# Where the operands of three matrix products lie in SBUF, modulo 256 bytes, and the order of their parts

## The chip, the cores and the metric

The kernel runs on one core of a Trainium2 chip. The metric is device time in microseconds (us). Engine names are those of the profile: PE is the matrix engine (TensorE), PEld its weight loads, DVE the vector engine, ACT the scalar engine, POOL GpSimd, SP the engine that issues most DMAs.

## The reference: one layer of a streaming encoder

A layer for 1024 new frames (prompt) and 64 frames of a running stream (sample), 1088 frames in all, in float32. Cut to what matters:

```
proj = rmsnorm(x) @ w_in                       # 1024 -> 5120
cb, cc, ch, q, k, v, ga, gb = split(proj)
ya = (cb * causal_conv(cc * ch)) @ w_conv_out  # 512 -> 1024
o  = band_attend(q, k, v, rel_bias)            # 8 heads of 64, own chunk + 8 earlier
yb = o @ w_attn_out                            # 512 -> 1024
x  = x + (sigmoid(ga) * ya + sigmoid(gb) * yb) @ w_out
x  = x + (silu(h @ w1) * (h @ w3)) @ w2        # h = rmsnorm(x), 1024 -> 2816 -> 1024
y  = rmsnorm(x)
```

## The kernel before

**Two-part operands.** Every float32 operand of a large product is kept as two parts of the type fp32r: *high* is ACT's cast of the value (L128), *low* is what DVE's subtraction leaves (L129); both are written by `split`. A product is then three matmuls: high x high, high x low, low x high. Each matmul on PE is a weight load (128 columns of 4 bytes) and a stream of 272 or 512 columns; the weight load of the next matmul runs while the present one streams.

**Where weight parts live.** `slots` (L147) hands out one part in a tile of the pool `ws` (eight tiles of 512 floats) and the other in one of eight slots of the row `low`: slot s begins at float 512 s + `at`. All tiles of `ws` have the same address modulo 256 bytes, and all slots with one `at` have the same. `pair` puts high into `ws` and low into `low`, `moving_pair` (v and the output projection, `at` 24) the other way round.

**The stages, in order of time.** (1) From 11 us: the value projection v, nine tiles of frames; xn (the normed frames, by 128) is the weight, w_v streams, 512 columns, eight blocks of 128 in depth (`v_tile`, L515 to L517: high x high, low x high, high x low). A tile's transposes (L459) stand between. (2) From 69 to 344 us: q, k, the convolution's inputs and most of gate b by a seven-product scheme (`run`, L269, 272 columns). (3) 344 to 573 us: ten blocks of the gates (`gate`, `product`, L333 to L335: four quarters of the frames of 272 columns, eight blocks deep), and between their matmuls attention: scores (L907, L908), softmax (DVE L865, ACT L875), transposes (L954), weighted values (`values`, L979: v is the weight, the transposed probabilities `pt` stream). The tile scheduler sets how the two interleave from their order in the program and their waits. Weights of a gate block, and of the next product after it, are loaded by SP and split by ACT and DVE ahead of use (`next_w`, `prep`). (4) 573 to 670 us: ya and yb, also by `product`, four blocks deep, `at` 40. (5) 670 to 771 us: the output projection in two halves of 512 columns (`wo_half`, `token_product`, L1163 to L1168: the merged activations `mg` are the weight, w_out streams). Frames tile 8, with 64 frames, takes two matmuls a block (L1167, L1168). The second half also adds the residual, norms and transposes. (6) To 1230 us: w_ff1 and w_ff3 by `run`. (7) To 1462 us: w_ff2 (L1682, 512 columns; L1509 for tile 8) and the final norm.

**Distances.** For a matmul that streams from address m while the weights of the next matmul are loaded from address w, call (w - m) modulo 256 bytes its distance. In the program as it is placed, the three matmuls of one block of depth have these distances, in the order of the lines:

| product | before | columns |
|---|---|---|
| v, and the output projection | 96, 192, 0 | 512 |
| weighted values | 64 | 512 and 256 |
| gates, quarters 0 and 2 | 96, 224, 0 | 272 |
| gates, quarters 1 and 3 | 192, 0, 192 | 272 |
| ya and yb, quarters 0 to 3 | 0, 0, 96; 192, 192, 32; 128, 128, 224; 64, 64, 160 | 272 |
| `run` (six matmuls a block) | 0, 192, 96, 0, 224, 192 | 272 |
| w_ff2 | 0, 0, 0 | 512 |

Of the kernel before, what the change touches and what calls it, by code (L numbers as in the profile page):

```python
# [8 lines left out]
F32 = mybir.dt.float32  # L9
# [6 lines left out]
P = 128  # L16
D = 1024
KD = D // P
# [15 lines left out]
HN = HT // 2  # L34
# [32 lines left out]
def encoder_kernel(ctx: ExitStack, tc: tile.TileContext, ins, outs):  # L67
    nc = tc.nc
    mm = nc.tensor.matmul
# [74 lines left out]
    def slots(nm, at):  # L144
        taken[0] += 1
        a = taken[0] % 8 * 512 + at
        return ws.tile([P, 512], F32R, tag="w", name=f"w{nm}"), low[:, a : a + 512]  # L147

    def pair(nm, at=0):
        return [t.rearrange("p (k n) -> p k n", k=4) for t in slots(nm, at)]  # L150

    def moving_pair(nm):
        lo, hi = slots(nm, 24)
        return hi, lo

    def quarters(nm):
        return Quarters(
# [146 lines left out]
    def prep(upto):  # L304
        while prep.n < min(upto, len(plan)):
            plain_load(prep.n)
            ld, kt, at = plan[prep.n]
            w = []
            for k in range(0, kt, 4):
                nm = f"p{prep.n}_{k}"  # L310
                hi, lo = pair(nm, ld.get("at", 0))
                split(hi, lo, ld["raw"][:, k : k + 4, at : at + P])
                w.append((hi, lo))
            plan[prep.n] = w
            prep.n += 1
# [10 lines left out]
    def product(out, w, x, o, n):  # L326

        kt = 4 * len(w)
        for k in range(kt):
            a, b = (t[:, k % 4] for t in w[k // 4])  # L330
            p, q = x.at(0, k, o, n), x.at(1, k, o, n)
            first, then = (q, p) if x is xn and o // HN % 2 == 0 else (p, q)
            mm(out, a, first, start=k == 0, stop=False)  # L333
            mm(out, a, then, start=False, stop=False)  # L334
            mm(out, b, p, start=False, stop=k == kt - 1)  # L335

    PIECES = [(j * HN, HN) for j in range(4)]
# [1 line left out]
    for g, m in GATES:  # L339
        if m % 2 == 0:  # L340
            base = (C_GA if g == "a" else C_GB) + m * P
            ld = {"src": w_in[:, base : base + 2 * P], "w": 2 * P}
# [10 lines left out]
    xn = quarters("xn")  # L353
# [53 lines left out]
    wv = []  # L407
# [99 lines left out]
    def v_tile(i):  # L507
        t0, n = TT[i]
        pv = bank1("BD", f"pvv{i}")[:, 0]
        for k in range(KD):  # L510
            if i == 8:
                a, b = xs8[:, k, :TS], xs8[:, k, TS:]
            else:
                a, b = xn.at(0, k, column(i), P), xn.at(1, k, column(i), P)
            mm(pv[:n], a, wv[k][0], start=k == 0, stop=False)  # L515
            mm(pv[:n], b, wv[k][0], start=False, stop=False)
            mm(pv[:n], a, wv[k][1], start=False, stop=k == KD - 1)  # L517
        put_v(slot(VST, D), pv, n, t0 if t0 < TP else TP + CACHE, nc.gpsimd)
        if t0 >= TP - CACHE:
            v32 = slot(V32, ATT)  # L520
            act.copy(v32[:n], pv[:n])
            if t0 < TP:
                dst = outs["cache_v_prompt"][t0 - (TP - CACHE) : t0 - (TP - CACHE) + n]
            else:
                dst = outs["cache_v_sample"][CACHE - TS :]
            nc.gpsimd.dma_start(dst, v32[:n])
# [278 lines left out]
    at_pool = att_stack.enter_context(tc.tile_pool(name="at_pool", bufs=2, reuse_waits="tile"))  # L805
# [115 lines left out]
    def transposed(h, t, s):  # L921
        tp = patt.tile([P, 2, 512], F32, tag="att", name=f"t{h}_{t}").rearrange("p a b -> p (a b)")
        if t == 8:
            pt = at_pool.tile([P, 2, 5, TS], F32R, tag="pts", name=f"pts{h}", bufs=1)
            for i in range(4):
                nc.tensor.transpose(
                    tp[:, i * TS : (i + 1) * TS], s[:TS, i * P : (i + 1) * P], ident[:TS, :TS]
                )
            nc.tensor.transpose(tp[:TS, 512 : 512 + TS], s[:TS, 512:576], ident[:TS, :TS])
            split(pt[:, 0, :4, :], pt[:, 1, :4, :], tp[:, : 4 * TS].rearrange("p (b t) -> p b t", t=TS))  # L930
            split(pt[:TS, 0, 4, :], pt[:TS, 1, 4, :], tp[:TS, 512 : 512 + TS])
            pts[h, 4] = pt

            sm = sums.pop(h)
            vec.reciprocal(sm, sm)
            tr = patt.tile([P, 2, 512], F32, tag="att", name=f"rt{h}")[:9, 0, :P]
            nc.tensor.transpose(tr, sm, ident)
            rows = at_pool.tile([P, P], F32, tag="rows", name=f"rows{h}", bufs=1)[:9]
            act.copy(rows, tr)
            for e in range(2):  # L940
                nc.gpsimd.dma_start(
                    rc_d[h, e * HT : e * HT + 512].rearrange("(t p) -> t p", p=P), rows[4 * e : 4 * e + 4]
                )
                c = e * HT + 512
                nc.gpsimd.dma_start(rc_d[h : h + 1, c : c + 32], rows[8:9, 32 * e : 32 * e + 32])
            return
        g, j = divmod(t, 2)
        if j == 0:
            pts[h, g] = at_pool.tile([P, 2, 6, 256], F32R, tag="pt", name=f"pt{h}_{g}")
        pt = pts[h, g]  # L950
        nb = min(t + 1, 5)
        b0 = t - nb + 1 - max(0, 2 * g - 4)
        for i in range(nb):
            nc.tensor.transpose(tp[:, i * P : (i + 1) * P], s[:, i * P : (i + 1) * P], ident)  # L954
        src = tp[:, : nb * P].rearrange("p (b t) -> p b t", t=P)
        js = slice(j * P, (j + 1) * P)
        split(pt[:, 0, b0 : b0 + nb, js], pt[:, 1, b0 : b0 + nb, js], src)
# [101 lines left out]
    for i in range(4, len(GATES)):  # L1059
        gate_w[i] = next_w()  # L1060
        if i == len(GATES) - LAST:
# [5 lines left out]
            for nm, pad in (("u", 56), ("ob", 48)):  # L1067
                uo.tile([P, pad], F32, name=f"pad_{nm}")
                t = uo.tile([P, 2, 4 * T + 8], F32R, name=nm)[:, :, : 4 * T]
# [10 lines left out]
            for k, r in zip((2, 3), late_r):  # L1080
                o = ob.t[:, 0, k].bitcast(F32)
                with tc.issue_after(u_ld.ins):
                    nc.sync.dma_start(o, o_d[k * P : (k + 1) * P])
                    ld = rc_load(r, k)
# [12 lines left out]
    for m0 in range(0, 8, 2):  # L1097
        for m in (m0, m0 + 1):
# [3 lines left out]
            for o, n in PIECES:  # L1102
                t = sg["ga", m, o]
# [5 lines left out]
        for m in (m0, m0 + 1):  # L1109
# [3 lines left out]
            for o, n in PIECES:  # L1113
                t, z = sg.pop(("ga", m, o)), sg.pop(("gb", m, o))
# [7 lines left out]
                h, a = o // HT, 512 - o % HT  # L1122
# [34 lines left out]
    def token_product(ps, i, x, kt, w, first=True, last=True):  # L1157

        for k in range(kt):
            wh, wl = w(k)  # L1160
            f, e = first and k == 0, last and k == kt - 1
            if i < 8:
                mm(ps, x(k, 0), wh, start=f, stop=False)  # L1163
                mm(ps, x(k, 1), wh, start=False, stop=False)  # L1164
                mm(ps, x(k, 0), wl, start=False, stop=e)  # L1165
            else:
                mm(ps, x(k, None), wh, start=f, stop=False)  # L1167
                mm(ps, x(k, None), wl, start=False, stop=e)  # L1168
# [21 lines left out]
    if True:  # L1190
# [7 lines left out]
        for i in ORDER:  # L1198
            t0, n = TT[i]
            xt = wp.tile([P, D], F32, tag="xg", name=f"xr{i}")[:, :512]  # L1200
            nc.sync.dma_start(xt[:n], x_rows(i)[:, :512])
            ps = bank2("BD", f"wo0_{i}")[:, 0]
# [369 lines left out]
    for n in range(1, len(names)):  # L1572
# [7 lines left out]
        if 2 <= n < 18:  # L1580
            nm, src = (("k", ck), ("v", cvv))[(n - 2) // 8]
            a = (n - 2) % 8 * 56
# [21 lines left out]
    bufs = {(hp, "hs"): 1, (hp, "snap"): 3, (hp, "sa"): 4, (hp0, "snap"): 1, (hp0, "sa"): 1}  # L1604
# [30 lines left out]
    q = 0  # L1635
    for b, ks in enumerate(blocks):
        first, final = b == 0, b == len(blocks) - 1
        nk = blocks[b + 1] if not final else []
        for g in range(2):
            ps = {}  # L1640
# [27 lines left out]
            for si, js in turns:  # L1668
                p, ht = STEPS[si], hts[base + si]
# [99 lines left out]
```

## Time and profile before

| | |
|---|---|
| median of 3 runs | 1471.76 us (1471.53 to 1471.95) |
| span of the profiled execution | 1470.3 us |
| PE busy | 1455.5 us, 99%, 10176 matmuls |
| PEld busy | 1366.9 us, 93% |
| DVE busy | 983.1 us, 67% |
| ACT busy | 679.7 us, 46% |
| DMA | 260 MB, 177 GB/s on average |

The profiled execution's own time is its span, 1470.3 us; 1.46 us of the median lie outside it. How to read the views: a group's row gives line, engine, operation, out<-in, tile sizes, count, busy time and the mean of one. A row by source line gives the shortest, median and longest of one in ns. A timeline row gives start, length and count; successive matmuls overlap in the timeline, since a matmul's row lasts until its last result is written, and the next has then begun to stream. What a matmul costs is the distance of its start from the next one's start, which is here called its spacing.

### The profile page before, as it was taken

The numbers are of one execution on the slowest core, as the hardware profiler recorded it, in microseconds if no ns is written. First come the engines' busy times: TensorE is split into PE (matmuls) and PEld (weight loads), VectorE is DVE, ScalarE is ACT, GpSimd is POOL, SyncE is SP. The second block draws the span as 40 slices with busy tenths as digits, with TensorE's granted clock in tenths as the row PEclk, the third lists the DMA queues.
The fourth block names the chain that finished last, engine by engine and source line by source line (L and its number), as shares of the span: only waits on it lengthen the run. The fifth ranks groups of instructions, "written<-read, shape, count | busy, mean of one in ns | idle before, by whom it ended". The sixth has DMA issues, their size and how long they took to land.

```text
span 1470.3 us, 26411 instructions
## 1 busy us (share of the span) xinstructions
PE 1455.5 (99%) x10176; PEld 1366.9 (93%) x10176; DVE 983.1 (67%) x1856; ACT 679.7 (46%) x1391; POOL 136.5 (9%) x249
## 2 busy tenths in 40 slices
PE   8999999999999999999999999999999999999997
PEld 6899999999989899998889999999999999888886
DVE  7975565641677775753588767666666768957677
ACT  7654333332777776531355444444444445512223
POOL 1400010001111111000100111110011111000000
PEclk9999999999999999999999999999999999999999
DMA  8687522237776657434432443443344448867686
GB/s 280 185 274 227 182 78 94 66 111 228 209 192 180 182 172 244 158 126 136 154 108 80 153 168 139 168 150 123 122 153 168 147 168 305 286 228 245 219 265 208
DMA packets 163133, 260.26 MB, mean 177 GB/s; under 512 B 18784, under 2 KB 98848, under 8 KB 163008
## 3 DMA queue, kind: packets, MB, share of 16 engines
q1 hardware_dynamic: 142080, 192.79, 41.6%
q0 software_dynamic: 19776, 63.70, 12.1%
q10 hardware_dynamic: 1152, 2.10, 0.4%
q8 instruction: 80, 1.31, 0.4%
q14 instruction: 45, 0.37, 0.1%
HBM read 170.67 MB, written 89.70 MB: 177 GB/s over the span
## 4 chain that ended last, share of the span: by engine, by line
PE 92%; DVE 3%; DMA 3%; ACT 1%; issue 1%; SPq 1%; ACTq 0%; DVEq 0%
PE Ab L269 9%; PE Aa L269 8%; PE A L1682 8%; PE Db L269 4%; PE Da L269 4%; PE D L1682 4%; PE Agb L269 2%; PE Bb L269 2%; PE Ba L269 2%; PE B L1682 2%; PE wo L1163 2%; PE wo L1165 2%; PE wo L1164 2%; PE g L335 2%; PE g L334 2%; PE g L333 2%
## 5 line engine op out<-in xcount | busy, mean ns | idle before, releaser
L333 PE MATMUL g<-xn,wp 128*128 128x272 f32 x320 | 93.7, 293 | 0.0
L335 PE MATMUL g<-xn,low 128*128 128x272 f32 x320 | 93.4, 292 | 0.0
L334 PE MATMUL g<-xn,wp 128*128 128x272 f32 x320 | 92.7, 290 | 0.0
L128 ACT CAST ring<-w2r 128x512 fp32r<-128x512 f32 (+1 forms) x78 | 43.2, 588 | 98.4 <-PE A L1682 50.7
L865 DVE CUSTOM_DVE_ANT_0 p<-s,bb 128x640 f32<-128x640 f32 (+5 forms) x72 | 47.5, 660 | 38.5 <-DMA qd<-q_d 26.2
L1682 PE MATMUL A<-ring,low 128*128 128x512 f32 x264 | 72.3, 389 | 0.0
L1682 PE MATMUL A<-ring,ht 128*128 128x512 f32 x264 | 72.3, 390 | 0.0
L129 DVE TENSOR_TENSOR low<-rawa,wa 128x512 fp32r<-128x512 f32 x55 | 37.7, 687 | 41.7 <-ACT wa L128 41.7
L335 PEld LDWEIGHTS g<-xn,low 128*128 128x128 f32 x320 | 60.3, 188 | 0.5
L333 PEld LDWEIGHTS g<-xn,wp 128*128 128x128 f32 x320 | 60.3, 188 | 0.5
L334 PEld LDWEIGHTS g<-xn,wp 128*128 128x128 f32 x320 | 60.2, 188 | 0.5
L1682 PEld LDWEIGHTS A<-ring,ht 128*128 128x128 f32 x264 | 49.4, 188 | 10.6 <-ACT acc L1692 0.4
L1682 PEld LDWEIGHTS A<-ring,low 128*128 128x128 f32 x264 | 49.6, 188 | 10.3
L269 PE MATMUL Ab<-tt,wb 128*128 128x272 f32 x352 | 57.8, 285 | 1.3 <-ACT wb L128 1.3
L129 DVE TENSOR_TENSOR ring<-w2r,ring 128x512 fp32r<-128x512 f32 (+1 forms) x78 | 49.0, 646 | 13.4 <-ACT ring L128 13.2
L269 PE MATMUL Ab<-mg,wb 128*128 128x272 f32 x352 | 58.0, 285 | 0.0
L269 PE MATMUL Aa<-tt,wa 128*128 128x272 f32 x352 | 57.8, 285 | 0.0
L269 PE MATMUL Aa<-mg,wa 128*128 128x272 f32 x352 | 57.7, 285 | 0.0
L875 ACT ACTIVATE p<-p,mx 128x640 f32<-128x640 f32 (+5 forms) x72 | 50.8, 706 | 11.4 <-DVE mx L865 10.1
L128 ACT CAST wa<-rawa 128x512 fp32r<-128x512 f32 x55 | 34.0, 621 | 47.4 <-PE Ab L269 33.3
L128 ACT CAST wb<-rawb 128x512 fp32r<-128x512 f32 x55 | 34.0, 620 | 38.7 <-PE Aa L269 24.5
L1163 PE MATMUL wo<-low,mg 128*128 128x512 f32 x128 | 50.9, 397 | 0.0
(554 smaller groups left out, 4547.9 us busy)
## 6 DMA issues: line engine op xcount, KB each, us to landing
h_d<-hq POOLq DMA_DIRECT2D x44, 512.0 KB, 4.4
ht<-h_d SPq DMA_DIRECT2D x77, 256.0 KB, 3.9
low<-h_d SPq DMA_DIRECT2D x77, 256.0 KB, 3.7
h_d<-hq_early POOLq DMA_DIRECT2D x29, 512.0 KB, 4.6
rawa<-in_w_ff SPq DMA_DIRECT2D x11, 1024.0 KB, 6.2
rawb<-in_w_ff SPq DMA_DIRECT2D x11, 1024.0 KB, 5.5
w2r<-in_w_ff SPq DMA_DIRECT2D x11, 1024.0 KB, 7.9
qd<-q_d SPq DMA_DIRECT2D x32, 272.0 KB, 4.1
```

The source lines that it names most:

```text
L128: a = act.copy(hi, src)
L129: b = vec.tensor_tensor(lo, src, hi.bitcast(F32), op=ALU.subtract)
L269: newest[0] = mm(t[:, j, :HN], w[:, k, :], x[p][:, k, l, j * HN : (j + 1) * HN], start=p in (1, 2, 7) and k == 0 and n == 0, stop=k == 3 a ...
L333: mm(out, a, first, start=k == 0, stop=False)
L334: mm(out, a, then, start=False, stop=False)
L335: mm(out, b, p, start=False, stop=k == kt - 1)
L865: vec.tensor_tensor_reduce(out=s if len(ps.shape) == 2 else s.rearrange("p (a b) -> p a b", a=2), in0=ps, in1=bias if len(ps.shape) == 2 e ...
L875: act.activation(s, s, AF.Exp, bias=mx, scale=-1.0, accum_out=sm)
L1163: mm(ps, x(k, 0), wh, start=f, stop=False)
L1164: mm(ps, x(k, 1), wh, start=False, stop=False)
L1165: mm(ps, x(k, 0), wl, start=False, stop=e)
L1682: mm(t, ht[k][:, j, x], w[:, l], start=p in (1, 2, 7) and k == 0 and n == 0, stop=k == len(ks) - 1 and n == 2, skip_group_check=p in (6, 5 ...
```

## The change

Four edits.

1. `moving_pair` (v and the output projection) now puts high into `ws` and low into `low`, with `at` 48 instead of 24. In `v_tile` and `token_product` the order becomes high-high, high-low, low-high (the first word for the weights).
2. Gate weights (the products with eight blocks of depth) are swapped: high into `low`, low into `ws`, and their `at` is 44 instead of 0. The last gate block's slot in `low` (floats 3116 to 3627) and the slot of the first block of ya (3624 to 4135, `at` 40) then share four floats, so four columns of the last gate block's last block of depth hold other numbers when they are read.
3. `product` no longer streams xn's low part first in the even quarters of the gates.
4. A tile of 16 floats in front of `pt` moves the probabilities by 64 bytes.

The distances as the changed program is placed; the others stay:

| product | before | after |
|---|---|---|
| v, and the output projection | 96, 192, 0 | 0, 0, 0 |
| weighted values | 64 | 0 |
| gates, quarters 0 and 2 | 96, 224, 0 | 144, 96, 144 |
| gates, quarters 1 and 3 | 192, 0, 192 | 80, 32, 80 |

```diff
     def moving_pair(nm):
-        lo, hi = slots(nm, 24)
-        return hi, lo
+        return slots(nm, 48)
...
                 nm = f"p{prep.n}_{k}"
-                hi, lo = pair(nm, ld.get("at", 0))
+                hi, lo = pair(nm, ld.get("at", 44))
+                if kt == KD:
+                    hi, lo = lo, hi
                 split(hi, lo, ld["raw"][:, k : k + 4, at : at + P])
...
             p, q = x.at(0, k, o, n), x.at(1, k, o, n)
-            first, then = (q, p) if x is xn and o // HN % 2 == 0 else (p, q)
-            mm(out, a, first, start=k == 0, stop=False)
-            mm(out, a, then, start=False, stop=False)
+            mm(out, a, p, start=k == 0, stop=False)
+            mm(out, a, q, start=False, stop=False)
             mm(out, b, p, start=False, stop=k == kt - 1)
...
             mm(pv[:n], a, wv[k][0], start=k == 0, stop=False)
-            mm(pv[:n], b, wv[k][0], start=False, stop=False)
-            mm(pv[:n], a, wv[k][1], start=False, stop=k == KD - 1)
+            mm(pv[:n], a, wv[k][1], start=False, stop=False)
+            mm(pv[:n], b, wv[k][0], start=False, stop=k == KD - 1)
...
         g, j = divmod(t, 2)
+        if (h, t) == (0, 0):
+            at_pool.tile([P, 16], F32, name="pad_pt", bufs=1)
         if j == 0:
...
                 mm(ps, x(k, 0), wh, start=f, stop=False)
-                mm(ps, x(k, 1), wh, start=False, stop=False)
-                mm(ps, x(k, 0), wl, start=False, stop=e)
+                mm(ps, x(k, 0), wl, start=False, stop=False)
+                mm(ps, x(k, 1), wh, start=False, stop=e)
```

The order of instructions moves in three places. PE at the start of v, before (`pvv8` and `pvv0` are the first two tiles of frames, `xt1_0` the transposes of the second; the streaming operand stands first, `low_95` or a tile `wv` of the pool `ws`, `xs8` and `xn00` are the weights):

```order
L515 MATMUL pvv8_236<-low_95,xs8_135 64x512
L459 MATMUL xt1_0_222<-ident_75,scr_111 128x128 x8
L516 MATMUL pvv8_236<-low_95,xs8_135 64x512
L517 MATMUL pvv8_236<-wv0_0_189,xs8_135 64x512
L515 MATMUL pvv8_236<-low_95,xs8_135 64x512
L516 MATMUL pvv8_236<-low_95,xs8_135 64x512
L515 MATMUL pvv0_301<-low_95,xn00_97 128x512
L517 MATMUL pvv8_236<-wv0_1_192,xs8_135 64x512
```

PE at the same place, now:

```order
L515 MATMUL pvv8_236<-wv0_0_189,xs8_135 64x512
L459 MATMUL xt1_0_222<-ident_75,scr_111 128x128 x8
L516 MATMUL pvv8_236<-low_95,xs8_135 64x512
L517 MATMUL pvv8_236<-wv0_0_189,xs8_135 64x512
L515 MATMUL pvv8_236<-wv0_1_192,xs8_135 64x512
L515 MATMUL pvv0_301<-wv0_0_189,xn00_97 128x512
L516 MATMUL pvv8_236<-low_95,xs8_135 64x512
L517 MATMUL pvv8_236<-wv0_1_192,xs8_135 64x512
```

`low_95` held the high part before and holds the low part now: the part that DVE writes is needed by the second matmul of a block, where it was needed by the third.

DVE in attention, heads 6 and 7, before (`low_95<-rawp10` and `rawp10,wp11` are the splits of the first two weight blocks of ya; `p` softmax rows, `pt` the low parts of transposed probabilities, `ca`, `co` the sums behind the weighted values):

```order
L883 TENSOR_TENSOR co6_0_6006<-ca6_0_6005 64x256
L129 TENSOR_TENSOR low_95<-rawp10_6698,wp10_0_6700 128x512
L865 ISA p6_5_6040,mx6_5_6045<-s6_5_6039,bb_3689 128x640
...
L865 ISA p6_8_6138,mx6_8_6143<-s6_8_6137,bb_3689 64x576
L865 ISA mx6_8_6143 64x1
L129 TENSOR_TENSOR pt6_3_6147<-t6_6_6146,pt6_3_6147 128x5x128
```

DVE at the same place, now:

```order
L882 TENSOR_TENSOR ca6_1_6079<-pv6_3_6074,ca6_1_6079 64x512
L129 TENSOR_TENSOR low_95<-rawp10_6699,wp10_0_6701 128x512
L883 TENSOR_TENSOR co6_1_6080<-ca6_1_6079 64x256
...
L865 ISA p6_8_6139,mx6_8_6144<-s6_8_6138,bb_3689 64x576
L865 ISA mx6_8_6144 64x1
L129 TENSOR_TENSOR low_95<-rawp10_6699,wp11_0_6824 128x512
L935 RECIPROCAL sm2_3694<-sm2_3694 128x9
L129 TENSOR_TENSOR pt6_3_6148<-t6_6_6147,pt6_3_6148 128x5x128
```

The first split moves behind three softmaxes; the second, which stood behind the last softmax of head 7, moves ahead into the end of head 6, in front of a split that transposed probabilities wait for.

SP in attention, before (`rawp10` and `rawp12` are the first weights of ya and of yb, `qd7`, `kd7`, `vd7` the queries, keys and values of head 7):

```order
L835 DMA qd7_1_5952<-q_d_87 64x1088 x2
L886 DMA o_d_92<-co5_0_5681 64x256
L301 DMA rawp10_6698<-in_w_conv_out 128x4x256
L844 DMA kd7_5955<-k_d_88 64x512
```

SP, now:

```order
L835 DMA qd7_1_5953<-q_d_87 64x1088 x2
L886 DMA o_d_92<-co5_0_5682 64x256
L844 DMA kd7_5956<-k_d_88 64x512 x3
...
L1005 DMA o0_6277<-o_d_92 128x1088
L300 DMA rawp10_6699<-in_w_conv_out 128x4x256
L300 DMA rawp12_6887<-in_w_attn_out 128x4x256
```

The load of ya's first weights moves behind all loads of head 7.

## The prediction

> **What bounds the kernel now.** First the page: the share of busy time, and the chain of work that ended last.
>
> ```profile
> span 1470.3 us, 26411 instructions
> PE 1455.5 (99%) x10176; PEld 1366.9 (93%) x10176; DVE 983.1 (67%) x1856; ACT 679.7 (46%) x1391; POOL 136.5 (9%) x249
> PE 92%; DVE 3%; DMA 3%; ACT 1%; issue 1%; SPq 1%; ACTq 0%; DVEq 0%
> ```
>
> PE is 92% of the chain. So time goes away where matmuls follow each other more closely, and nearly nothing else can give any. Next, how closely: the chain in w_ff2 (start, length, count), and two starts of the output projection in the timeline, 24 matmuls apart (the rows between are left out).
>
> ```profile
> 1299.80 4.08 PE D L1682 x18
> 1303.88 8.16 PE A L1682 x36
> ```
> ```profile
> 683.64 0.39 PE L1163 MATMUL wo<-low,mg 128*128 128x512 f32 x1
> ...
> 689.13 0.39 PE L1163 MATMUL wo<-low,mg 128*128 128x512 f32 x1
> ```
>
> w_ff2: 8.16 us / 36 = 226.7 ns from start to start. Output projection: 5.49 us / 24 = 228.8 ns. Both are matmuls of 512 columns with 128 weights, back to back. The rows by source line (shortest, median, longest of one, in ns) show where the 2 ns sit; a matmul's row is its spacing plus a tail of 162 ns (389 - 226.7 here), so differences of medians are differences of spacing.
>
> ```profile
> L1682 PE MATMUL A<-ring,ht x264: 389/389/497, 1230.4 to 1461.7; 128*128 128x512 f32 x132
> L1682 PE MATMUL A<-ring,low x264: 387/389/397, 1231.0 to 1462.3; 128*128 128x512 f32 x132
> ```
> ```profile
> L1163 PE MATMUL wo<-low,mg x128: 389/394/505, 672.6 to 770.0; 128*128 128x512 f32 x128
> L1164 PE MATMUL wo<-low,mg x128: 388/388/481, 672.9 to 770.2; 128*128 128x512 f32 x128
> L1165 PE MATMUL wo<-wo,mg x128: 388/391/401, 673.1 to 770.5; 128*128 128x512 f32 x128
> ```
> ```profile
> L515 PE MATMUL pvv<-low,xn x64: 391/394/481, 13.8 to 68.2; 128*128 128x512 f32 x64
> L516 PE MATMUL pvv<-low,xn x64: 388/388/497, 18.8 to 68.5; 128*128 128x512 f32 x64
> L517 PE MATMUL pvv<-wv,xn x64: 388/391/403, 19.2 to 68.7; 128*128 128x512 f32 x64
> ```
> ```profile
> L979 PE MATMUL pv<-pt,vd x144: 276/394/497, 378.2 to 549.6; 128*128 128x512 f32 x96, 128*128 128x256 f32 x48
> ```
>
> The reader is to see that medians go with distances and not with stages: v and the output projection lie 600 us apart and have 394, 388, 391 both, at distances 96, 192, 0; w_ff2, always at distance 0, has 389 throughout, the lowest sum of three. That the 0 among 96 and 192 has 391 says that the neighbours' distances count too. Weighted values, at 64, have 394.
>
> **The change part by part.** *Output projection.* Three matmuls cost 394 + 388 + 391 = 1173 now, 3 x 389 = 1167 at distance 0: 6 ns a block of depth, 128 blocks (8 tiles of frames x 8 x 2 halves): -0.77 us. By the timeline (228.8 - 226.7 = 2.1 ns x 384) it is -0.81. All of it is on PE in the chain. What follows the second half is less simple:
>
> ```profile
> L269 PE MATMUL Ab<-tt,wb 128*128 128x272 f32 x352 | 57.8, 285 | 1.3 <-ACT wb L128 1.3
> ```
> ```profile
> 781.75 3.03 PE Bb L269 x24
> ...
> 784.83 0.41 issue
> 785.24 0.72 DVE sb L1367
> 785.96 1.20 DVE tt L129 x2
> ```
>
> At 794 us PE waits 1.3 us at the end of a run of DVE work, and that run begins when PE ends `Bb`. It begins earlier by as much as PE comes earlier, but only while DVE is free then: it stood idle some 0.4 us ("issue" in the chain) before 785.24. The second half's 0.38 us fits in that, with little left; I take half of it, 0.2 us, as lost (bounds 0 and 0.38).
>
> *v.* The same 6 ns x 64 blocks: -0.38 us. The order adds a wait: the part that DVE writes is needed by the second matmul of a block.
>
> ```profile
> 11.21 1.32 PE L459 MATMUL xt<-ident,scr 128*128 128x128 f32 x8
> 12.47 0.44 PE L516 MATMUL pvv<-low,xs 128*64 128x512 f32 x1
> 13.08 0.44 PE L517 MATMUL pvv<-wv,xs 128*64 128x512 f32 x1 [0.16 <-DVE wv L129]
> 13.36 0.39 PE L515 MATMUL pvv<-low,xs 128*64 128x512 f32 x1
> ...
> 18.30 0.39 PE L517 MATMUL pvv<-wv,xs 128*64 128x512 f32 x1
> 18.82 0.50 PE L516 MATMUL pvv<-low,xn 128*128 128x512 f32 x1
> ```
> ```profile
> 12.34 0.68 DVE L129 TENSOR_TENSOR wv<-wv,low 128x512 fp32r<-128x512 f32 x1
> ...
> 18.09 0.68 DVE L129 TENSOR_TENSOR xn<-xt,xn 128x512 fp32r<-128x512 f32 x1
> ```
>
> DVE's part is there at 13.02. Before, the matmul at 12.47 filled the wait; now PE stands until 13.08 with everything behind it in its queue, and that matmul runs later: +0.23 us, one spacing. It comes back at 18.82: that matmul needed xn's low part, which DVE ends at 18.77, and started 0.52 after the one ahead of it, not 0.23. Now the part read there is w_v's, long there, and xn's is needed one matmul later. So 0 (bounds -0.1 and +0.23).
>
> *Weighted values.* Of 144 rows the 48 short ones lie below the median, so the 96 long ones are at 394 or above; at distance 0 I take 389: 5 ns x 96 = -0.48 us. Bounds: 0, should attention's waits swallow it, and -0.7 with the 256-column ones gaining as much.
>
> *Gates.* 960 matmuls whose distances become 144, 96, 144 and 80, 32, 80. No matmul before steadily runs at 80 or 144. Nearest rows: the gates themselves after attention has ended, then ya, which visits 0, 32, 64, 96, 128, 160, 192 and 224 in the same loop, then `run`.
>
> ```profile
> L333 PE MATMUL g<-xn,wp x52: 283/288/291, 549.8 to 569.9; 128*128 128x272 f32 x52
> L334 PE MATMUL g<-xn,wp x51: 283/288/290, 549.9 to 569.7; 128*128 128x272 f32 x51
> L335 PE MATMUL g<-xn,low x52: 285/287/392, 549.7 to 569.8; 128*128 128x272 f32 x52
> ```
> ```profile
> L333 PE MATMUL ya<-u,wp x128: 282/287/296, 572.9 to 656.5; 128*128 128x272 f32 x128
> L334 PE MATMUL ya<-u,wp x128: 283/288/292, 573.0 to 656.7; 128*128 128x272 f32 x128
> L335 PE MATMUL ya<-u,low x128: 282/287/289, 573.1 to 656.8; 128*128 128x272 f32 x128
> ```
> ```profile
> L269 PE MATMUL Ab<-mg,wb 128*128 128x272 f32 x352 | 58.0, 285 | 0.0
> L269 PE MATMUL Ab<-mg,low 128*128 128x272 f32 x176 | 36.1, 286 | 0.0
> ```
>
> 863 for three in the gates, 862 in ya: at 272 columns quite different sets of distances give one price. I take 0. Lower bound: `run`'s mean of 285.3 against 287.7: -2.4 ns x 960 = -2.3 us. Upper: all at 291, the longest row of L333: +3.3 ns x 960 = +3.2 us. The swap itself costs nothing: ACT and DVE write as many bytes as before, only elsewhere, and xn has lain ready since v.
>
> *What moves in attention.* On DVE one split of ya's weights (0.69 us) goes ahead of a split of `pt`; another moves back behind three softmaxes. On SP, the load of ya's first weights moves behind head 7's loads, which come earlier by one issue.
>
> ```profile
> 513.66 0.69 DVE L129 TENSOR_TENSOR low<-rawp,wp 128x512 fp32r<-128x512 f32 x1 [0.20 <-DMA vd<-v_d]
> ...
> 543.64 1.28 DVE L129 TENSOR_TENSOR low<-rawp,wp 128x512 fp32r<-128x512 f32 x2
> ```
> ```profile
> L301 SPq DMA_DIRECT2D rawp<-in_w_conv_out x4: 368/410/532, 494.5 to 587.8; - x4
> ```
>
> ya begins at 572.9, 59 us after the first split: the later load and splits cost nothing. The 0.69 us on DVE is behind gate matmuls that fill PE; 0, with bounds of -0.69 and +0.69 (it stands in head 6 and leaves head 7).
>
> The sum: -0.77 + 0.2 - 0.38 - 0.48 = -1.43 us. The span becomes 1470.3 - 1.4 = 1468.9, and with the 1.46 us that the median lies above it, 1471.76 - 1.4 = 1470.4 us. That is 0.1%; about 0.2% (2.9 us) is what a measurement of this kernel can tell from no change.
>
> **The rivals.** *A, distances do nothing.* The medians could follow the order of the parts (first, second, third of a block) or the tiles. For: each distance stands always at the same place in v and the output projection. Against: w_ff2 has the same three-part blocks and 389 at each place. Result 1471.8. The Trainium skill (TensorE: Matmul & The Clock Gate, "Step-by-step: what each phase is for") says the same in another way: PE reads weights and the streaming operand through two independent ports, so loading the next weights takes nothing from the running matmul; by that rule edits 1, 2 and 4 give nothing. This trace does not bear it out: 389 against 394 for equal matmuls. Chance 0.17.
>
> *B, the gates get shorter too,* down to `run`'s 285.3: -2.3 - 1.4 = -3.7, 1468.1 us. For: `run` shows that 272 columns can be faster, at multiples of 32 as well. Against: `run` alternates between two banks of PSUM, and ya, which like the gates stays in one, never gets there with any of its distances. Chance 0.18.
>
> *C, the gates get longer.* 80 and 144 are 16 off a multiple of 32, as no steady distance was before, and if a weight load that begins so holds up each streaming matmul, the gates go up to 291: +3.2 - 1.4 = +1.8, 1473.6 us. It decides from 1.5 ns a matmul, where the gates (960) eat what 512 columns (672 matmuls) gain. For: the longest rows of the gates and ya, 291 to 296, show that such spacings occur. Against: their medians do not move over eight distances. Chance 0.15.
>
> **How the numbers follow.** Forecast 0.50, 1470.4, its own range 1469.2 to 1471.6 (bounds of the loss, of the weighted values and of attention). A 0.17, B 0.18, C 0.15. The range of 8 in 10 takes in A, B to a little past its point and most of C: 1467.8 to 1473.2. Faster by over 0.2% (under 1468.8): two thirds of B and a few hundredths of the forecast, 0.15. Slower by over 0.2% (over 1474.7): a fifth of C and some for a mishap in attention, 0.04. Within: 0.81.
>
> **What would show it.** In the profile after: L1163 to L1165 and L515 to L517 with medians of 389 at all three places, L979's median at 389; L333 to L335 at 287 to 288 outside attention; the wait at 13 us about 0.2 longer and the one at 18.8 gone; the 1.3 us at 794 us longer by 0.2. Wrong would be: places that keep 394 (A), gates at 285 (B) or 290 and above (C), or new waits of PE in heads 6 and 7.

## The result: 3.2 us slower, where 1.4 us less was forecast

| | before | after |
|---|---|---|
| median of 12 runs each, taken together | 1471.56 us (1470.64 to 1473.03) | 1474.76 us (1474.25 to 1477.66) |
| ratio, 95% interval | | 1.0024 (1.0017 to 1.0032) |
| span of the profiled execution | 1470.3 us | 1473.7 us |

The time lies above the range of 1467.8 to 1473.2. A run's time is some 2.1 us more than its span (the 1.46 us that the prediction added came from a median and a span of different executions), and spans of one kernel differ: some thirty executions of the kernel before, taken later, have a median span of 1469.1 us. The 1470.3 of the profile is thus 1.2 us on the long side, and the 1473.7 is 1.0 above its kernel's median. Stage sums that differ by less than 0.5 us say nothing by themselves.

The page after, the same lines as before:

```profile
span 1473.7 us, 26396 instructions
PE 1456.6 (99%) x10176; PEld 1367.0 (93%) x10176; DVE 985.1 (67%) x1856; ACT 679.7 (46%) x1391; POOL 136.1 (9%) x249
PE 94%; DVE 2%; DMA 2%; ACT 1%; issue 1%; SPq 0%; ACTq 0%; DVEq 0%
```

PE's busy time grew by 1.1 us and the span by 3.4: part of the loss is longer matmuls, the larger part is time in which PE stood still. The starts of the stages after, by source line (first and last start are the last two times), tell where:

```profile
L333 PE MATMUL g<-xn,low x320: 282/288/392, 343.9 to 574.9; 128*128 128x272 f32 x160
L333 PE MATMUL ya<-u,wp x128: 282/287/291, 575.3 to 658.9; 128*128 128x272 f32 x128
L1165 PE MATMUL wo<-wo,mg x128: 389/393/502, 675.2 to 773.5; 128*128 128x512 f32 x128
L1166 PE MATMUL wo<-low,mg x128: 387/397/479, 675.4 to 773.7; 128*128 128x512 f32 x128
L1167 PE MATMUL wo<-wo,mg x128: 390/393/397, 675.7 to 774.0; 128*128 128x512 f32 x128
L1684 PE MATMUL A<-ring,ht x264: 389/389/498, 1233.4 to 1465.1; 128*128 128x512 f32 x132
```
```profile
L333 PE MATMUL g<-xn,wp x320: 282/288/392, 344.4 to 572.5; 128*128 128x272 f32 x160
```

The second fence is the gates' row of the kernel before. The gates begin 0.5 us earlier than before (343.9 against 344.4), ya 2.4 later (575.3 against 572.9): gates and attention take 2.9 us more. The output projection ends 3.5 later (774.0 against 770.5), so it takes 1.1 more; w_ff2 begins 3.0 later, so 0.5 is given back between them, which is no more than such sums differ by anyway. Two things are to be explained, 2.9 us in attention and 1.1 in the output projection, and neither was in the forecast.

**Attention.** The waits of PE from 495 to 560 us (waiting line, what it waited for, sum, times, longest), after and then before:

```profile
PE t L956 <- DVE pt L129: 1.9, 2, 1.7
PE t L956 <- DVE mx L865: 0.6, 1, 0.6
PE s L907 <- DVE mx L865: 0.2, 1, 0.2
```
```profile
PE t L954 <- DVE pt L129: 0.4, 2, 0.2
PE s L907 <- DVE mx L865: 0.2, 1, 0.2
```

A new wait of 1.7 us and one of 0.6. All waits of PE from 344 to 575 us sum to 3.3 us after and 1.1 before: 2.2 of the 2.9 us. Some 0.4 us more lie in the gates' own matmuls (below, under Gates); the last 0.3 is within what such sums differ by. The chain of waits after, followed back from the transposes that began at 523.57, names the cause of the first wait:

```profile
515.56 4.92 DMA rawp<-in_w_conv_out
520.48 0.02 issue
520.50 0.02 ACT wp L128
520.52 0.14 issue
520.67 0.02 ACTq L815
520.69 0.34 issue
521.03 0.92 ACT p L875 x2
521.95 0.03 issue
521.97 0.70 ACT pt L128
522.67 0.02 issue
522.70 0.83 DVE pt L129
523.53 0.04 issue
523.57 0.77 PE t L956 x5
```

It begins with the load of ya's first weights. SP issued it at 515.56 (494.54 before), it landed 4.92 us later, ACT's cast of it started at 520.50, and behind that cast in ACT's queue stood a softmax's exponential and the cast of transposed probabilities, behind these DVE's subtraction, and behind that PE. ya itself needed the weights 55 us later. In time order on ACT:

```profile
518.07 0.59 ACT L881 COPY ca<-pv 64x512 f32<-64x512 f32 x1
520.50 0.62 ACT L128 CAST wp<-rawp 128x512 fp32r<-128x512 f32 x1 [1.84 <-DMA rawp<-in_w_conv_out]
521.03 0.83 ACT L875 ACTIVATE p<-p,mx 128x640 f32<-128x640 f32 x1
```

ACT stood 1.84 us at the cast. The Trainium skill (Perfetto Trace Analysis, "Tensor Engine Instruction (MATMUL, LD_WEIGHTS)") says that ACT and DVE are strict first-in, first-out. The trace agrees: the exponential, which did not need the load, began 0.53 us after the cast and not before it.

The second wait, of 0.6 us at 544 us, has a cause of the same kind on DVE. The same chain holds a load of `rc` (the reciprocals of the softmax's sums), and DVE's waits from 500 to 560 us show the instruction that stood for it, the multiplication of `o` by `rc`:

```profile
538.44 3.46 DMA rc<-rc_d
```
```profile
DVE o L1007 <- DMA rc<-rc_d: 1.0, 1, 1.0
```

SP issued this load 4.0 us later than before (538.44 for 534.45). The multiplication began at 541.92, the softmax queued behind it at 543.13, and PE's transposes, which waited for that softmax, at 544.10. Before, the same multiplication did not wait.

### The profile page after: what moved, and what is told of

It is laid out like the page before. It is cut to its first block, busy times and chain, and to the rows that moved or that the text cites. A ratio compares the mean times of both kernels' runs of the same rounds, so it can differ in the third digit from the quotient of the medians.

```text
span 1473.7 us, 26396 instructions
## 1 busy us (share of the span) xinstructions
PE 1456.6 (99%) x10176; PEld 1367.0 (93%) x10176; DVE 985.1 (67%) x1856; ACT 679.7 (46%) x1391; POOL 136.1 (9%) x249
## 4 chain that ended last, share of the span: by engine, by line
PE 94%; DVE 2%; DMA 2%; ACT 1%; issue 1%; SPq 0%; ACTq 0%; DVEq 0%
PE Ab L268 9%; PE Aa L268 8%; PE A L1684 7%; PE Db L268 4%; PE Da L268 4%; PE D L1684 4%; PE g L334 2%; PE g L333 2%; PE g L335 2%; PE Agb L268 2%; PE Ba L268 2%; PE Bb L268 2%; PE B L1684 2%; PE wo L1166 2%; PE wo L1165 2%; PE wo L1167 2%
## 5 line engine op out<-in xcount | busy, mean ns | idle before, releaser
L333 PE MATMUL g<-xn,low 128*128 128x272 f32 x320 | 93.7, 293 | 0.0
L335 PE MATMUL g<-xn,wp 128*128 128x272 f32 x320 | 93.3, 292 | 0.0
L334 PE MATMUL g<-xn,low 128*128 128x272 f32 x320 | 92.9, 290 | 0.0
L334 PEld LDWEIGHTS g<-xn,low 128*128 128x128 f32 x320 | 60.2, 188 | 0.6
L335 PEld LDWEIGHTS g<-xn,wp 128*128 128x128 f32 x320 | 60.3, 188 | 0.4
L333 PEld LDWEIGHTS g<-xn,low 128*128 128x128 f32 x320 | 60.2, 188 | 0.5
```

The source lines that it names most:

```text
L333: mm(out, a, p, start=k == 0, stop=False)
L334: mm(out, a, q, start=False, stop=False)
```

## The experiments

All times are medians in us, with those of the kernel before that ran beside them on the same chip.

| run | time | before | ratio, 95% interval |
|---|---|---|---|
| e1_swap_alone | 1473.15 | 1471.30 | 1.0010 (1.0001 to 1.0019) |
| e2_after_no_swap | 1472.10 | 1471.30 | 1.0003 (0.9993 to 1.0012) |
| e3_v_out_alone | 1472.04 | 1471.30 | 1.0002 (0.9993 to 1.0011) |
| e4_one_class | 1489.03 | 1471.30 | 1.0115 (1.0099 to 1.0132) |
| e5_split_late | 1472.52 | 1471.22 | 1.0008 (0.9999 to 1.0017) |
| e6_stream_one | 1472.80 | 1471.22 | 1.0009 (1.0000 to 1.0018) |
| e7_weights_one | 1474.70 | 1471.22 | 1.0022 (1.0013 to 1.0031) |
| e8_both_one | 1473.10 | 1471.22 | 1.0013 (1.0004 to 1.0022) |
| e9_out_one | 1470.45 | 1471.31 | 0.9993 (0.9984 to 1.0002) |
| e10_apart, one run | 1472.21 | 1471.31 | |
| e11_gap16, one run | 1477.00 | 1471.31 | |
| e12_gap24, one run | 1477.84 | 1471.31 | |

### The wait in attention: e1, e2, e5

*The swap alone.* Edit of the kernel before:

```diff
                 hi, lo = pair(nm, ld.get("at", 0))
+                if kt == KD:
+                    hi, lo = lo, hi
```

> The kernel before, with only the gates' two weight parts swapped (high where low was). Theory 1 (the swap alone moves the load of ya's first weights behind head 7's loads, ACT and DVE wait in their queues for it, and PE waits with them): PE gaps of over 0.7 us in heads 6 and 7 that sum to some 2 to 2.6 us, and a time 1.8 to 2.8 us over the kernel before; the gate matmuls outside of waits at 287 to 288. Theory 2 (the loss in attention comes from the gates' distances of 144, 96, 144 and 80, 32, 80, or from the other order of their products, which this kernel does not have): no such gaps, time within 0.5 us of the kernel before.

Measured +1.85 us. The load is issued at 514.72, and the waits of PE from 495 to 560 us hold the new one:

```profile
PE t L956 <- DVE pt L129: 1.5, 2, 1.3
PE s L909 <- DVE mx L867: 0.2, 1, 0.2
```

Theory 1 holds for the first of the two waits, a little smaller than in the changed kernel (1.3 against 1.7 us, at an ACT wait of 1.4). Its sum of 2 to 2.6 us was too high: the second wait, of 0.6 us, is not there (DVE stands 0.3 us for `rc`, and PE doesn't see it). The profiled execution is one of the shortest of this kernel, 1472.15 us where the eleven reach 1476.52, so the waits of the others may be longer. The gates' distances of 144, 96, 144 and 80, 32, 80 and the other order of their products, which this kernel does not have, are not needed for the first wait.

*The changed kernel without the swap.*

```diff
-                if kt == KD:
-                    hi, lo = lo, hi
```

> The changed kernel without the swap of the gates' parts; everything else of the change is kept, the shifted place of the parts too. Theory 1 (the swap moves the load): the load is issued ahead of head 7's loads again, PE's gaps of 1.9 and 0.8 us in heads 6 and 7 are gone, and the time is 2.2 to 2.8 us under the changed kernel's, so some 0.5 to 1.0 us over the kernel before (output projection +1.1, v +0.5, q and k -0.7, weighted values -0.24). Theory 2 (the gates' distances or the order of their products): the gaps and the +3.2 us stay.

Measured 0.80 us over the kernel before where the changed kernel has 3.20: the swap is worth 2.4 us. The load is back at 493.69 and PE's waits are those of before (0.4 and 0.2 us):

```profile
493.69 0.53 SPq L300 DMA_DIRECT2D rawp<-in_w_conv_out  x1
```

*The swap kept, the split moved.* The load stays late; the two casts on ACT and the two subtractions on DVE that split it go behind head 7's second softmax (`late` holds the exponential and the maximum of `p7_1`):

```diff
+                if prep.n == 10:
+                    with tc.issue_after(late[0]), tc.issue_after(late[1]):
+                        split(hi, lo, ld["raw"][:, k : k + 4, at : at + P])
+                else:
```

> The changed kernel, the swap and the late load kept, with one thing moved: ACT and DVE split ya's first weights only behind the second softmax of head 7 instead of in head 6, so that nothing that PE needs is queued behind the wait for the load. Theory 1 (it is this wait in ACT's and DVE's queues that PE sees): PE's gaps of 1.9 and 0.8 us in heads 6 and 7 go, and with them 1.9 to 2.7 us against the changed kernel, which leaves about 1471.9 to 1472.8 us. Theory 2 (head 7's earlier loads or the gates' distances cost it): the time stays at 1474 to 1475 us, and the gaps stay.

Measured 1472.52, 1.30 over the kernel before: 1.9 of the 3.2 us less. The load is issued as late as in the changed kernel (515.54), ACT comes to it at 525.75 without standing, and PE's waits from 495 to 560 us are

```profile
PE s L914 <- DVE mx L870: 0.5, 2, 0.4
PE t L963 <- DVE pt L129: 0.4, 2, 0.2
```

The 1.7 and the 0.6 us are gone, and a wait of 0.4 us at 543 us is new. It does not lie where the moved instructions now stand: just before it DVE had waited for `rc` again, with a softmax behind it.

```profile
DVE o L1014 <- DMA rc<-rc_d: 0.5, 1, 0.5
```

So neither head 7's earlier loads nor the gates' distances cost the 1.7 us: what cost it was two instructions, one on ACT and one on DVE, that waited ahead of others in their queues.

### The addresses: e3, e4, e6 to e12

*v and the output projection alone.* The diff of `moving_pair`, `v_tile` and `token_product`, nothing else.

> The kernel before with the edits of v and the output projection alone (operands 0 apart mod 256, products high-high, high-low, low-high). By the prediction's theory (distance 0 gives the shortest spacing): medians of 389 at all six places, time 1.0 to 1.2 us under the kernel before. By the theory formed from the result (equal distances are not enough: what costs is that the address mod 256 changes from one matmul to the next, 224, 128, 224 in the streaming operand here): medians of 393, 397, 393 as in the changed kernel, output projection +1.1, v +0.5, time some 1.0 to 1.6 us over the kernel before.

Measured +0.74 us, with medians of 393, 397, 393 in the output projection. The medians refute the prediction's theory (389 at all places, 1.0 to 1.2 us less); of the time alone the interval still holds 1. The other theory came out a little low. v's medians are longer in the same way; those of the changed kernel, whose v is the same:

```profile
L515 PE MATMUL pvv<-wv,xn x64: 389/394/503, 13.7 to 68.5; 128*128 128x512 f32 x64
L516 PE MATMUL pvv<-low,xn x64: 387/397/478, 16.8 to 68.7; 128*128 128x512 f32 x64
L517 PE MATMUL pvv<-wv,xn x64: 390/393/475, 18.9 to 68.9; 128*128 128x512 f32 x64
```

Yet v as a whole took no longer. From its first matmul to the start of q, five executions of kernels with v as before took 57.6 to 58.0 us, and four with v as changed 57.6 to 58.2. The two parts of that are apart: from the third tile of frames on v takes 43.9 us for 43.0, and up to it 13.8 to 14.3 for 14.6 to 15.0. The new order takes less time at the head; which waits or instructions make that up was not followed.

What is left is which property of w_ff2 makes its 389. It has all four parts, high and low of both operands, at one address modulo 256 bytes, 224. Equal distances were one consequence of that. In the changed kernel the distances are equal, but the addresses move from matmul to matmul. e4, e6, e7, e8 set these apart (in bytes modulo 256, in the order of the lines; medians of the output projection in ns):

| kernel | weights at | streaming operand at | medians | sum |
|---|---|---|---|---|
| before | 224, 128, 224 | 32, 32, 224 | 394, 388, 391 | 1173 |
| after | 224, 224, 128 | 224, 128, 224 | 393, 397, 393 | 1183 |
| e6 | 224, 128, 224 | 224 | 398, 396, 394 | 1188 |
| e7 | 224 | 32, 32, 224 | 396, 397, 393 | 1186 |
| e8 | 224 | 224 | 390, 390, 390 | 1170 |
| e4, e9 | 224 | 224 | 389, 389, 389 | 1167 |
| e10 | 32 | 224 | 394, 394, 394 | 1182 |

From start to start, the spacings of the three sum to 681 ns in e4 and e9, 688 before, 696 after and 700 in e6, e7 and e10; the sums of the rows follow them to 4 ns.

*e4*, of the kernel before:

```diff
-        t = t.rearrange("p (k n) -> p k n", k=4)[:, :, : 2 * (HT + 8)]
+        t = t.rearrange("p (k n) -> p k n", k=4)[:, :, : 2 * (HT + 32)]
...
-    def pair(nm, at=0):
+    def pair(nm, at=8):
...
-        lo, hi = slots(nm, 24)
+        lo, hi = slots(nm, 8)
...
-                hi, lo = pair(nm, ld.get("at", 0))
+                hi, lo = pair(nm, ld.get("at", 8))
```

> The kernel before with the pitch between an operand's high and low part widened by 24 floats and the weights' pairs placed so that high and low parts of both operands all start at 224 mod 256 in v and the output projection, as they do in w_ff2; the order of the products stays. Theory 3 (the address must stay at one class from matmul to matmul): the medians of v and of the output projection come down to 389 at all three places, together 1.1 us less there. Theory 4 (v and the output projection differ from w_ff2 for another reason than addresses): medians stay at 388 to 394 and over. The pitch also changes the addresses in the gates and in the matmuls of the conv units, 5,800 matmuls: at 1 ns each, up to 6 us either way, which no theory here gives.

Theory 3 held: 389 at all three places, in v too. From start to start the output projection lost 0.84 us and v 0.75 (against e1's execution), 0.3 of the latter from the third tile on. The kernel is 17.7 us slower all the same, for what the edit does elsewhere: `run` took 18.8 us more over its 5,880 matmuls, 3.2 ns each. Its group of 352, whose mean was 285 before:

```profile
L269 PE MATMUL Ab<-mg,wb 128*128 128x272 f32 x352 | 59.1, 289 | 0.0
```

The placement that is best for a stream of 512 columns is the worst of those tried for `run`. Two things changed for `run` here: its streaming operand has its parts 0 apart instead of 160, and the low part of its weights lies at 224 instead of 192. e7 below has the first alone, on `mg`, and it costs 1.1 ns a matmul; so the pitch alone does not explain 3.2.

*e6*: `lo, hi = slots(nm, 8)` in `moving_pair` alone, so that only the streaming operand keeps its address.

> The kernel before with only the second operand's parts of v and the output projection moved by 16 floats, so that both parts of the streaming operand start at 224 mod 256; the weights stay at 224, 128, 224, the order of the products as before. Theory S (only the streaming operand's address must keep its class): medians of 389 at all three places of the output projection, 0.8 us less there and 0.4 in v. Theory W (the weights' must too): the matmuls around the one with weights at 128 stay longer, three medians that sum to 1172 or more. Theory D (it is the distance of the next weights from the streaming operand alone, 0 best): spacings grow only around the one distance that is not 0.

Theory S is refuted, and so is theory D, since two of the three distances are 0 and no place has 389:

```profile
L1163 PE MATMUL wo<-low,mg x128: 389/398/506, 671.7 to 770.3; 128*128 128x512 f32 x128
L1164 PE MATMUL wo<-low,mg x128: 390/396/477, 671.9 to 770.6; 128*128 128x512 f32 x128
L1165 PE MATMUL wo<-wo,mg x128: 390/394/398, 672.2 to 770.8; 128*128 128x512 f32 x128
```

*e7*: `mg = quarters("mg", 32)`, the wider pitch for the output projection's activations alone, so that only the weights keep their address.

> The kernel before with a wider pitch between the high and the low part of the activations of the output projection alone, so that all of its weights lie at 224 mod 256; the streaming operand stays at 32, 32, 224, and v is not touched. Theory W (the weights' class is what counts): medians of 389 at all three places of the output projection, 0.8 us less. Theory S (the streaming operand's class): the two steps of the streaming operand between 32 and 224 stay longer than 389, the one that stays at 32 is at 389.

Theory W is refuted too, with 396, 397, 393; theory S was wrong in its second half also, since the step that stays at 32 has no 389. One operand held still is worse than before, where both moved. The 3.5 us come mostly from w_ff1 and w_ff3, which stream the same tile `mg` with its wider pitch (+2.7 us from start to start, against e3's execution). The matmuls of `run` that stream `mg` have a mean spacing of 124.5 ns instead of 123.4, the others are unchanged.

*e8*: both edits, and the 16 floats ahead of `pt`.

> The kernel before with the last two edits together and the shift of the weighted values' second operand to distance 0; gates, order of products and everything else as before. If both operands must keep their class: 389 at all three places of the output projection, 0.8 us less there, weighted values 0.2 less, v as in the run with the streaming operand alone: 1.0 to 1.6 us under the kernel before, 1469.7 to 1470.3. If the saving is taken back by the wait at 794 us, 0.3 less of it.

390 at all three places, so the output projection did what was expected, but the time is 1.9 us up: `mg` costs w_ff1 and w_ff3 its 2.7 us again, and v, with a streaming operand held still and weights that move, takes 0.6 more from the third tile on (43.65 us for 43.0).

*e9* takes both of these away: the wider pitch is a second view of `mg` that the output projection alone uses, and the streaming operand's 8 applies there alone.

```diff
+    mg_t = mg.t
+    mg = Quarters({gh: hl_view(base_of[f"mg{gh[0]}{gh[1]}"], 32) for gh in mg_t})
...
-    ax = mg.t
+    ax = mg_t
...
-                hi, lo = moving_pair(f"o{hf}_{kq}_{k}")
+                hi, lo = moving_pair(f"o{hf}_{kq}_{k}", 8)
```

In e9 and the three after it the next stage writes frames tile 8 into the old view of `mg` before tiles 3 and 7 are read in the second half; in these two tiles the low parts of 24 columns (16 in e11, 8 in e12; in e10 32, and the high parts of 16) then hold other numbers. As many instructions run on as many bytes.

> The kernel before, in which only the output projection sees its activations with the wider pitch (the next stage reads the same tile with the old one), the streaming operand's parts lie at 224 there and nowhere else, and the weighted values' second operand is at distance 0. Both operands of the output projection lie at 224 throughout; v, gates and the conv units have the addresses of the kernel before. If one address class for both operands is what makes 227 ns, the output projection has 389 at all places and gives 0.8 us, the weighted values 0.2: 1.0 us less, 1470.2 beside 1471.2, and the next stage loses nothing (it lost 2.8 in the run with the pitch for all). If the gain is taken back by the wait at 794 us: 0.5 less instead of 1.0.

```profile
L1174 PE MATMUL wo<-low,mg x128: 387/389/501, 671.8 to 768.4; 128*128 128x512 f32 x128
L1175 PE MATMUL wo<-low,mg x128: 387/389/477, 672.0 to 768.6; 128*128 128x512 f32 x128
L1176 PE MATMUL wo<-wo,mg x128: 388/389/397, 672.2 to 768.8; 128*128 128x512 f32 x128
```

0.86 us less, 1.0 expected; the interval still holds 1. From start to start the output projection gives 0.8 us (against e1's execution). PE's wait behind it, at 794 us, lasts 1.4 us instead of e1's 1.1; that this takes back a part of the gain is not shown, since e10, whose output projection takes 1.3 us more than e1's, also waits 1.4. By its median it is the shortest of all kernels here, but a version that doesn't overwrite those columns was not built.

*e10*: e9 with the two parts of the weights 16 floats further, so that neither operand moves from matmul to matmul and the two are 64 apart.

> The last kernel with the output projection's weights moved by 16 floats, both parts: all weights at 32, all streaming operands at 224, so that neither changes its class from matmul to matmul, but the two are 64 apart. If constancy of each operand is enough, whatever the distance, the three medians are 389. If the distance has to be 0 as well, as the prediction took it, they are 391 or more.

```profile
L1174 PE MATMUL wo<-low,mg x128: 393/394/504, 671.4 to 770.1; 128*128 128x512 f32 x128
L1175 PE MATMUL wo<-low,mg x128: 392/394/477, 671.6 to 770.3; 128*128 128x512 f32 x128
L1176 PE MATMUL wo<-wo,mg x128: 390/394/400, 671.9 to 770.5; 128*128 128x512 f32 x128
```

394 at each place. So for these matmuls operands that stay are not enough (e10), and distance 0 is not enough either (after, e6): of the placements tried, only both operands at one address modulo 256 bytes, in every matmul, gave 389 or 390. One other distance, 64, was tried with operands that stay, and one address, 224, at distance 0.

*e11 and e12*: e9 with a pitch of `HT + 16` and `HT + 24` for all other activations, that is, high and low part 192 and 224 apart modulo 256 instead of 160.

> The kernel with the one-class output projection and, for all other activations, a pitch wider by 8 floats: the high and the low part of what streams in the conv units and of the gates' streaming operand are 192 apart mod 256 instead of 160. At distance 0 they cost 3.2 ns a matmul more (5,880 matmuls, 18.8 us). If each step's price depends on the two classes it joins, the sum over the six steps changes by some ns and the time by some us, either way; if only distance 0 is bad, within 1 us of the kernel before.

> The same with the two parts 224 apart mod 256. As for the last: a change by some us either way if each step's price depends on the classes it joins, within 1 us if only distance 0 is bad.

5.7 and 6.5 us over the kernel before, 6.6 and 7.4 over e9. Of that, `run` took 6.1 and 6.6 us in their traces, 1.0 and 1.1 ns a matmul. Theirs are single runs. So distance 0 of the two parts is not the only bad one: parts 0 (on `mg` alone, e7), 192 and 224 apart all cost about 1.1 ns a matmul of `run` against the 160 of the kernel before, with the weights where they were. The other 2 ns of e4's 3.2 came only with the weights' low part moved too. Why is not settled.

## Why the prediction was wrong

**The step that failed for most of it** is the one on attention: "ya begins at 572.9, 59 us after the first split: the later load and splits cost nothing", with bounds of 0.69 us, and with it "the swap itself costs nothing". The swap alone cost 1.85 us (e1), and 2.4 with the other edits (e2). The prediction asked when the result is needed, and priced the split's own work; it did not ask who is queued behind the split while that waits for its load. The trace of before and the order of instructions had what was needed for the first wait. In that order the load of ya's first weights moves next to that of yb's first, which was issued at 515.91; a load of this kind takes 4.8 us (issue to landing, before):

```profile
515.91 0.41 SPq L301 DMA_DIRECT2D rawp<-in_w_attn_out  x1
```
```profile
rawp<-in_w_conv_out SPq DMA_DIRECT2D x4, 512.0 KB, 4.8
```

So, issued one issue earlier, it lands at 515.5 + 4.8 = 520.3. ACT's copy `ca`, behind which the cast now stands, ended at 519.0:

```profile
518.43 0.58 ACT L881 COPY ca<-pv 64x512 f32<-64x512 f32 x1
```

That gives an estimated wait of 1.3 us on ACT; 1.8 came, with a softmax and a cast behind it that PE needed. The prediction named "new waits of PE in heads 6 and 7" as what would prove it wrong, and left about 0.01 for it (0.04 for any loss over 0.2%, of which a fifth of C's 0.15 is 0.03).

**The second step that failed** is "3 x 389 = 1167 at distance 0" for the output projection and v. Expected -0.77 and -0.38 us; the output projection took +1.1, 1183 ns a block of depth instead of 1167, and v about 0: +0.9 for its spacing from the third tile on, and some -0.7 at its head, where the prediction had no gain beyond 0.1. That v came out even is luck: its spacing got longer where the forecast had it shorter, and the head made up for it. The reading that w_ff2's 389 comes from distance 0 rested on one stage that differed from the others in more than the distance. The sentence "the neighbours' distances count too" had the weak point in it, and it was not followed to a rival in which distance 0 is not enough.

**What it lost at 794 us.** Forecast +0.2, because PE would come there earlier; it came later. The runs don't bear the step out or refute it: the group `Ab<-tt,wb` waited 1.3 us before and 1.1 after, but also 1.1 in e1, whose output projection is that of before, and 1.4 in e9 and e10 alike, though that of e10 takes 2.1 us longer. What sets this wait stays open.

**Weighted values:** forecast -0.48, measured -0.1 to -0.2 from start to start; mean and busy time of the 512-column ones went from 425 ns and 30.5 us to

```profile
L981 PE MATMUL pv<-pt,vd 128*128 128x512 f32 x96 | 30.4, 424 | 0.0
```

The median of L979's row (now L981) came to 393, not 389, although both operands stay at one address (0) and the distance is 0. That row holds the short matmuls too; those of 512 columns alone have 397 before and after. Unlike the others they stream two pieces of 256 columns; whether that is why, no run tells.

**Gates:** 0 was nearly right apart from the waits. After attention has ended, the three lines have 288, 287, 287, where they had 288, 288, 287:

```profile
L333 PE MATMUL g<-xn,low x60: 282/288/291, 549.8 to 574.9; 128*128 128x272 f32 x60
L334 PE MATMUL g<-xn,low x61: 283/287/400, 549.5 to 575.0; 128*128 128x272 f32 x61
L335 PE MATMUL g<-xn,wp x61: 283/287/289, 549.7 to 575.2; 128*128 128x272 f32 x61
```

The medians hide a small change: between neighbouring gate matmuls the mean from start to start, waits left out, went from 124.8 to 125.3 ns, some 0.4 us over 960. The other kernels with swapped gate parts, e1 and e5, have 125.2; e2, without the swap, has 125.0. So rivals B (285) and C (291) are both out. C's 1473.6 us came nearest to the time by luck: it asked for 3.3 ns a gate matmul, and 0.4 to 0.5 came. Rival A, that distances do nothing, is out by e10 against e9: the same instructions with the weights 64 bytes elsewhere, and 394 for 389. The rule of the Trainium skill beside it (TensorE: Matmul & The Clock Gate, "Step-by-step: what each phase is for": two independent ports, so that loading the next weights takes nothing from the running matmul) is not the whole of it here: where the weights lie changes the spacing of 227 ns by 5 to 6. By which mechanism, no run shows.

## What to carry to other kernels

When an edit moves a load, work out when it lands, find the instruction that waits for it, and read what stands behind that instruction on its engine: the slack (how late the load may come at no cost) is that of the first needed instruction in that queue, not that of the load's own result. An edit that only renames which half of a pair is which can move a load in a scheduler's order. And a spacing that one stage has is copied only with all that the stage has: here the addresses of all four parts, not their distances.

## What the runs showed of the hardware

- The spacing of back-to-back matmuls depends on addresses modulo 256 bytes: from 227 ns a matmul of 512 columns (e4, e9) to 233 (e6, e10), with as many matmuls of the same sizes.
- For the 272 columns of `run` the same choice goes the other way: high and low part of the streaming operand at equal addresses cost 1.1 ns a matmul (e7, `mg`), and 3.2 ns, 18.8 us in all, with the weights' low part moved to 224 as well (e4).
- ACT stood 1.84 us at a cast that waited for a load, and an exponential that didn't need the load began 0.53 us after it (after).
- In the two placements tried (e6, e7), an operand held at one address while the other moves is slower than both moving as they did before (1188 and 1186 against 1173, sums of three rows).
